# Wide products with a weight's high part, and down blocks placed among the next chunk's pairs, in a one-core decoder layer

## The chip, the cores and the metric

The kernel runs on one core of a Trainium2 chip. The metric is device time in microseconds (us). TensorE (PE in the profile; its weight loads are PEld) multiplies, VectorE (DVE) and ScalarE (ACT) do the elementwise work, GpSimd (POOL) a little of it, and SyncE's queue (SP) issues the DMAs.

## What is computed

A decoder layer in float32, with 512 tokens and 1024 channels: a half-step SwiGLU feed-forward layer (FFN), a token mixer (RG-LRU channels and stick-breaking attention), and a second FFN. Each FFN has 2816 hidden channels:

```python
def _swiglu(x, w_gate, w_up, w_down):
    return (jax.nn.silu(x @ w_gate) * (x @ w_up)) @ w_down

x = x + 0.5 * _swiglu(_rms_norm(x, ffn1_norm[l]), ffn1_w_gate[l], ffn1_w_up[l], ffn1_w_down[l])
... # mixer: proj = h @ w_in; RG-LRU group; attention heads; x = x + y @ w_out
x = x + 0.5 * _swiglu(_rms_norm(x, ffn2_norm[l]), ffn2_w_gate[l], ffn2_w_up[l], ffn2_w_down[l])
```

## The kernel before

**Number format.** Every operand is held as a high part in the rounded format fp32r and a low part (value minus high part). A product is three matmuls: high x high, high x low, low x high (`mm3`, L136 to L138).

**FFN.** The 2816 hidden channels are 22 blocks `f` of 128, taken as 11 pairs `p`, in `CHUNKS` of 6, 6, 6 and 4 blocks. The first three pairs (chunk 0) are plain: 8 k-tiles x 3 matmuls of 512 columns for gate and for up. The pairs 3 to 10 use Strassen's scheme in Winograd's form (`fast`, `matrix`): for a pair's gate matrix and its up matrix, 7 products each of 4 k-tiles x 3 matmuls of 256 columns (L371). Each matrix keeps two PSUM banks, `px` and `py`; a product accumulates on one of them, and behind each product either ScalarE copies the bank to SBUF (`keep`, L389) or VectorE adds it to what was kept (`add`, L394). The 14 products of a pair run in the order "g0 g1 u0 u1 g2 g3 u2 u3 g4 g5 u4 g6 u5 u6".

**Weights of a fast pair.** 1 MB each for gate and up comes in a `raw` buffer (3 buffers, L331). VectorE makes four sums (L334 to L338), ScalarE casts each of four groups to a high part (L357), VectorE subtracts for the low part (L358); high and low parts have 4 buffers each (`wh`, `wl`), which the down weights share.

**Operands of the fast pairs.** `operands()` builds them once for each FFN from the normed input, in four blocks `b` of 8 x 256 columns (L298 to L321), one buffer, high and low parts in separate tiles.

**Down.** At the end of a chunk come 8 down blocks, one for each 128 output channels (L427 to L447): up to 6 x 3 matmuls of 512 columns, then VectorE adds half of the result to `x` (L441).

**Mixer.** Of it the change touches the first projection's bank, and the stretch of the `v` projection: `norm_heads` (head norms of k; `r8k` on POOL, `natk` on VectorE), `yn.rsqrt` (`pst_r` on TensorE, `m_r` on VectorE, `r_r` on POOL), `turn` (transposes `ptk`), and `rnn_out`, which begins with `yn.spread` (four transposes of `r_r` into `pst_r`, L193) and makes `yrh` and `yrl` for the output projection `po`.

**Order.** Tiles and waits come from a scheduler that works at build time: the order on each engine follows the program order, moved by its own model, and then stands. `tc.issue_after(i)` puts the instructions traced in it behind `i` on their engine.

Of the kernel before, what the change touches and what calls it, by code (L numbers as in the profile page):

```python
# [15 lines left out]
P = 128  # L16
T = 512
# [13 lines left out]
TH = T // 2  # L31
WARM = 9
# [14 lines left out]
def hybrid_layer_kernel(  # L47
# [93 lines left out]
    class Normed:  # L141
# [5 lines left out]
        def add(self, xk, gain, j):  # L147
            n = self.name
            h = xpool.tile([P, T], F32R, tag="xh", name=f"xh_{n}{j}", bufs=8)
            high = nc.scalar.activation(h, xk, AF.Copy, scale=gain)  # L150
            l = xpool.tile([P, T], F32R, tag="xl", name=f"xl_{n}{j}", bufs=8)
            nc.vector.scalar_tensor_tensor(
                l, xk, gain, f32(h), op0=ALU.mult, op1=ALU.subtract
            )
            self.h[j], self.l[j] = h, l
            return high
# [11 lines left out]
        def rsqrt(self, dim, tag="y"):  # L168

            n = self.name  # L170
            pt = self.pt = bank(f"pst_{n}", tag)
            for b in range(NB):
                self.summed = nc.tensor.matmul(
                    pt[:, b : b + 1],
                    self.acc[:, b * P : (b + 1) * P],
                    ones[:, 0:1],
                    start=True,
                    stop=True,
                )
            m = stat.tile([P, NB], F32, tag="m", name=f"m_{n}")  # L180
            nc.vector.tensor_scalar(
                m, pt[:, 0:NB], 1.0 / dim, EPS, op0=ALU.mult, op1=ALU.add
            )
# [30 lines left out]
    def ffn(name, xn, wg, wu, wd, first, done):  # L214
        def products(f, between=None, tag="b"):
# [4 lines left out]
            pg, pu = (bank(f"{p}{n}", tag) for p in ("pg", "pu"))  # L220
            each = ((pg, gh, gl), (pu, uh, ul))
            order = [(e, k) for e in each for k in range(KD)]
            if f == 0:
                order = [(e, k) for k in range(KD) for e in each]
            for i, ((pt, wh, wl), k) in enumerate(order):
                s = slice(k * P, (k + 1) * P)
                mm3(pt, wh[:, s], wl[:, s], xn.h[k], xn.l[k], k == 0, k == KD - 1)
                if between and i == KD - 1:
                    between()
            return pg, pu  # L230

        if first:
            ahead = first()
            ahead.append(products(len(ahead), tag="y"))
        else:
            ahead = [products(0), products(1)]
            xn.rsqrt(D)
            ahead.append(products(len(ahead), xn.spread, "y"))
        rb = xn.rb
        with tc.tile_pool(name=f"ffn_{name}", bufs=1, reuse_waits="tile") as fp:  # L240
# [4 lines left out]
            def pair_tiles(p):  # L245
                n = f"{name}{p}"
                g = fp.tile([P, 4, TH], F32, tag="g", name=f"gg{n}", bufs=2)
                u = fp.tile([P, 4, TH], F32, tag="u", name=f"uu{n}")
                return g, u

            def split(u, p, i):

                n = f"{name}{p}"
                h = fp.tile([P, 2, T], F32R, tag=f"hh{i}", name=f"hh{n}")
                l = fp.tile([P, 2, T], F32R, tag=f"hl{i}", name=f"hl{n}")
                for t in range(2):
                    src = flat(u[:, 2 * t : 2 * t + 2, :])
                    nc.scalar.copy(h[:, t, :], src)
                    nc.vector.tensor_sub(l[:, t, :], src, f32(h[:, t, :]))
                return [(h[:, t, :], l[:, t, :]) for t in range(2)]  # L260
# [21 lines left out]
            def operands():  # L282
# [3 lines left out]
                def tiles(n):  # L286
                    if extra[0]:
                        extra[0] -= 1
                        i = extra[0]
                        return [fp.tile([P, 2, TH], F32R, tag=f"x{c}{i}", name=f"x{c}_{n}") for c in "hl"]  # L290
                    return [
                        xpool.tile([P, 2, TH], F32R, tag=f"x{c}", name=f"x{c}_{n}", bufs=8) for c in "hl"
                    ]

                for k in range(KD // 2):
                    n = f"s{name}{k}"

                    b = fp.tile([P, 8, TH], F32, tag="b", name=f"b{n}")  # L298
                    for kk, o in ((2 * k, b[:, 0:2, :][:, ::-1, :]), (2 * k + 1, b[:, 2:4, :])):
                        h, l = (f32(p[kk]).rearrange("p (c t) -> p c t", c=2) for p in (xn.h, xn.l))  # L300
                        nc.vector.tensor_add(o, h, l)
# [8 lines left out]
                    for s in (B11, B22, T2, T4):  # L310
                        if s == T4 and k % 2:
                            h, l, o = *operands.last, 1
                        else:
                            h, l = tiles(f"{n}_{s}")
                            o = 0
                        w = 1 if s == T4 else 2
                        if w == 1:
                            operands.last = h, l
                        src = b[:, s + 1 : s + 1 + w, :]
                        nc.scalar.copy(h[:, o : o + w, :], src)  # L320
                        nc.vector.tensor_sub(l[:, o : o + w, :], src, f32(h[:, o : o + w, :]))  # L321
                        for i in range(w):
                            held[k, s + i] = h[:, o + i, :], l[:, o + i, :]

            def matrix(w, c, p):
# [37 lines left out]
                px, py = (bank(f"p{i}{n}", "b")[:, :TH] for i in "xy")  # L363

                def product(pt, group, half, b, start):
                    wh, wl = get(group)
                    for k in range(KD // 2):
                        s = slice((half * 4 + k) * P, (half * 4 + k + 1) * P)
                        bh, bl = held[k, b]
                        for i, (l, r) in enumerate(((wh, bh), (wh, bl), (wl, bh))):  # L370
                            nc.tensor.matmul(  # L371
                                pt, l[:, s], r, start=start and k == 0 and i == 0,
                                stop=k == KD // 2 - 1 and i == 2, skip_group_check=True,
# [9 lines left out]
            def fast(p, i):  # L383

                g, u = pair_tiles(p)

                def keep(o, c):
                    def after(pt):
                        nc.scalar.copy(o[:, c, :], pt)  # L389
                    return after  # L390

                def add(o, c):
                    def after(pt):
                        nc.vector.tensor_add(o[:, c, :], pt, o[:, c, :])  # L394
                    return after

                def last_gate(pt):
                    nc.scalar.activation(g[:, 2, :], pt, AF.Silu, scale=-1.0)

                both = {}  # L400
                for c, w, o, end in (("g", wg, g, last_gate), ("u", wu, u, keep(u, 2))):

                    after = [keep(o, 0), add(o, 0), keep(o, 1), keep(o, 3), add(o, 3), add(o, 1), end]
                    steps, product = matrix(w, c, p)
                    both[c] = [(product, *z) for z in zip(steps, after)]

                for c in "g0 g1 u0 u1 g2 g3 u2 u3 g4 g5 u4 g6 u5 u6".split():
                    product, step, after = both[c[0]][int(c[1])]
                    product(*step)
                    after(step[0])  # L410
                    if c == "g5":
                        nc.scalar.activation(flat(g[:, 0:2, :]), flat(g[:, 0:2, :]), AF.Silu)
                        nc.scalar.activation(g[:, 3, :], g[:, 3, :], AF.Silu, scale=-1.0)
                nc.vector.tensor_mul(u[:, 0:2, :], u[:, 0:2, :], g[:, 0:2, :])
                nc.vector.scalar_tensor_tensor(
                    u[:, 2:4, :], u[:, 2:4, :], -1.0, g[:, 2:4, :], op0=ALU.mult, op1=ALU.mult
                )
                return split(u, p, i)

            f0 = 0  # L420
            for nf in CHUNKS:
                hs = []
                for i in range(nf // 2):
                    p = f0 // 2 + i
                    hs += (plain if 2 * p < PLAIN else fast)(p, i)
                last = f0 + nf == NF
                for k in range(KD):  # L427
# [20 lines left out]
                if f0 == 0:  # L448
                    operands()
                f0 += nf  # L450
# [216 lines left out]
    def rnn_out():  # L667
        yn.spread(same=True)
# [47 lines left out]
    def norm_heads(n, pts):  # L716
        nats = []
        for b in range(NB):
# [10 lines left out]
            nc.vector.scalar_tensor_tensor(  # L729
                heads(nat),  # L730
                heads(pts[b]),
                rb,
                r.unsqueeze(2).to_broadcast([P, NH, HD]),
                op0=ALU.mult,
                op1=ALU.mult,
            )
# [35 lines left out]
    def gate_and_recur(last):  # L772
# [7 lines left out]
    nk = norm_heads("k", pk)  # L780
# [322 lines left out]
```

## Time and profile before

| | us |
|---|---|
| median of 3 runs (907.25 to 907.58) | 907.39 |
| profiled execution | 907.71 |
| its span | 905.9 |
| TensorE busy | 899.7 |
| VectorE busy | 667.3 |
| ScalarE busy | 450.2 |

The span is that of the instructions; 1.8 us of the profiled execution lie around it. A busy TensorE here is a union of modelled matmul intervals, so its work is better read from the spacing of matmul starts.

### The profile page before, as it was taken

The numbers are of one execution on the slowest core, as the hardware profiler recorded it, in microseconds if no ns is written. First come the engines' busy times: TensorE is split into PE (matmuls) and PEld (weight loads), VectorE is DVE, ScalarE is ACT, GpSimd is POOL, SyncE is SP. The second block draws the span as 40 slices with busy tenths as digits, with TensorE's granted clock in tenths as the row PEclk, the third lists the DMA queues.
The fourth block names the chain that finished last, engine by engine and source line by source line (L and its number), as shares of the span: only waits on it lengthen the run. The fifth ranks groups of instructions, "written<-read, shape, count | busy, mean of one in ns | idle before, by whom it ended". The sixth has DMA issues, their size and how long they took to land.

```text
span 905.9 us, 13634 instructions
## 1 busy us (share of the span) xinstructions
PE 899.7 (99%) x5442; PEld 793.0 (88%) x5442; DVE 667.3 (74%) x998; ACT 450.2 (50%) x757; POOL 70.6 (8%) x60
## 2 busy tenths in 40 slices
PE   9999999999999999999999999999999999999998
PEld 8888899889998998877877677888899989998997
DVE  8699788648865859757698948499688657875663
ACT  6443455335542546365768834443356335642450
POOL 0000000000000005553140002200000000000000
PEclk9999999999999999999999999999999999999999
DMA  8531123512242122322131015322222422242102
GB/s 267 197 136 53 53 94 98 180 49 93 94 163 88 47 94 72 127 93 75 66 115 49 24 47 211 139 61 61 70 94 93 163 70 95 93 163 88 48 24 93
DMA packets 27600, 89.26 MB, mean 99 GB/s; under 512 B 2960, under 2 KB 6288, under 8 KB 23440
## 3 DMA queue, kind: packets, MB, share of 16 engines
q1 hardware_dynamic: 27392, 88.35, 28.8%
q8 instruction: 43, 0.70, 0.3%
q14 instruction: 21, 0.17, 0.1%
q10 hardware_dynamic: 144, 0.03, 0.0%
HBM read 86.28 MB, written 2.10 MB: 98 GB/s over the span
## 4 chain that ended last, share of the span: by engine, by line
PE 93%; DVE 3%; ACT 2%; issue 1%; POOL 1%; DVEq 0%; POOLq 0%; ACTq 0%
PE pxga L371 5%; PE pxgb L371 5%; PE pxub L371 5%; PE pxua L371 5%; PE pdb L138 4%; PE pdb L137 4%; PE pdb L136 4%; PE pda L138 4%; PE pda L137 4%; PE pda L136 4%; PE pygb L371 4%; PE pyga L371 4%; PE pyua L371 4%; PE pyub L371 4%; PE first_p L503 4%; PE po L136 2%
## 5 line engine op out<-in xcount | busy, mean ns | idle before, releaser
L137 PE MATMUL pdb<-hlb,h_db 128*128 128x512 f32 (+2 forms) x180 | 68.9, 386 | 0.0
L138 PE MATMUL pdb<-hhb,l_db 128*128 128x512 f32 (+2 forms) x180 | 68.9, 386 | 0.0
L137 PE MATMUL pda<-hla,h_da 128*128 128x512 f32 x176 | 68.0, 389 | 0.0
L138 PE MATMUL pda<-hha,l_da 128*128 128x512 f32 x176 | 67.9, 389 | 0.0
L136 PE MATMUL pdb<-hhb,h_db 128*128 128x512 f32 (+2 forms) x180 | 67.4, 385 | 0.0
L136 PE MATMUL pda<-hha,h_da 128*128 128x512 f32 x176 | 66.2, 389 | 0.0
L441 DVE SCALAR_TENSOR_TENSOR x<-pdb,x 128x512 f32<-128x512 f32 (+2 forms) x33 | 21.9, 672 | 49.8 <-PE pdb L138 49.8
L441 DVE SCALAR_TENSOR_TENSOR x<-pda,x 128x512 f32<-128x512 f32 x32 | 21.7, 686 | 39.8 <-PE pda L138 39.8
L126 ACT CAST h_da<-r_da 128x768 fp32r<-128x768 f32 (+1 forms) x28 | 24.1, 868 | 48.6 <-PE pda L137 20.8
L126 ACT CAST h_db<-r_db 128x768 fp32r<-128x768 f32 (+1 forms) x28 | 24.3, 868 | 45.2 <-PE pdb L137 23.3
L137 PEld LDWEIGHTS pdb<-hlb,h_db 128*128 128x128 f32 x180 | 33.8, 188 | 6.6
L136 PEld LDWEIGHTS pdb<-hhb,h_db 128*128 128x128 f32 x180 | 33.8, 188 | 6.5
L138 PEld LDWEIGHTS pdb<-hhb,l_db 128*128 128x128 f32 x180 | 33.8, 188 | 6.5
L137 PEld LDWEIGHTS pda<-hla,h_da 128*128 128x128 f32 x176 | 33.0, 188 | 6.7
L138 PEld LDWEIGHTS pda<-hha,l_da 128*128 128x128 f32 x176 | 33.1, 188 | 6.7
L136 PEld LDWEIGHTS pda<-hha,h_da 128*128 128x128 f32 x176 | 33.1, 188 | 6.6
L371 PE MATMUL pxgb<-xh_sb,l_gb 128*128 128x256 f32 x128 | 36.2, 283 | 0.0
L371 PE MATMUL pxga<-xh_sa,l_ga 128*128 128x256 f32 x128 | 36.2, 283 | 0.0
L371 PE MATMUL pxga<-xl_sa,h_ga 128*128 128x256 f32 x128 | 36.2, 283 | 0.0
L371 PE MATMUL pxgb<-xl_sb,h_gb 128*128 128x256 f32 x128 | 36.2, 283 | 0.0
L371 PE MATMUL pxua<-xh_sa,l_ua 128*128 128x256 f32 x128 | 36.2, 283 | 0.0
L371 PE MATMUL pxub<-xh_sb,l_ub 128*128 128x256 f32 x128 | 36.2, 283 | 0.0
(393 smaller groups left out, 3050.5 us busy)
## 6 DMA issues: line engine op xcount, KB each, us to landing
r_da<-in_wd SPq DMA_DIRECT2D x24, 384.0 KB, 3.4
r_db<-in_wd SPq DMA_DIRECT2D x24, 384.0 KB, 3.1
rga<-in_wg SPq DMA_DIRECT2D x8, 1024.0 KB, 5.0
rua<-in_wu SPq DMA_DIRECT2D x8, 1024.0 KB, 4.8
rgb<-in_wg SPq DMA_DIRECT2D x8, 1024.0 KB, 4.9
rub<-in_wu SPq DMA_DIRECT2D x8, 1024.0 KB, 4.8
r_o<-in_w_out SPq DMA_DIRECT2D x8, 512.0 KB, 3.5
r_gb<-in_wg SPq DMA_DIRECT2D x6, 512.0 KB, 3.3
```

The costliest lines, as they stand in the source:

```text
L126: nc.scalar.copy(hi, raw)
L136: nc.tensor.matmul(out_, wh, ah, start=start, stop=False)
L137: nc.tensor.matmul(out_, wh, al, start=False, stop=False)
L138: return nc.tensor.matmul(out_, wl, ah, start=False, stop=stop)
L371: nc.tensor.matmul(pt, l[:, s], r, start=start and k == 0 and i == 0, stop=k == KD // 2 - 1 and i == 2, skip_group_check=True,)
L441: nc.vector.scalar_tensor_tensor(x[k][:, t], pt[:, t], 0.5, x[k][:, t], op0=ALU.mult, op1=ALU.add)
L503: nc.tensor.matmul(pts[i], wp[i][:, s], xp[k], start=k == 0 and wp is hi and xp is n1.h, stop=k == KD - 1 and wp is lo,)
```

## The change

In each FFN, 10 of the 16 fast matrices become wide (`WIDE`: gate of the pairs 3 to 10, up of the pairs 6 and 9). An operand's high and low part now lie side by side, and a wide product is, for each k-tile, one matmul of 512 columns (the weight's high part with both parts) and one of 256 (the weight's low part with the high part) into half of the bank. The two halves are evicted as 512 columns and added once for each matrix by VectorE (1024 columns). SiLU is applied after g6 to all four quarters. The down blocks of the chunks 1 and 2 are issued among the products of the next chunk's first two pairs (`BETWEEN`: before the z-th product of pair i); the first pair of that chunk is split later (`SPLIT`). The blocks `b` move to the `raw` buffers; gate tiles have one buffer, and kept products two shared ones of double size. The second FFN takes the banks of its third block first; the mixer's first projection takes a bank of another group; `norm_heads` of k's last block and `rnn_out` are issued later.

```diff
+BETWEEN = [(0, 2), (0, 5), (0, 8), (0, 11), (1, 0), (1, 2), (1, 4), (1, 6)]
+SPLIT = (1, 8)
+LATE = 3
+WIDE = {p: "gu" if p in (6, 9) else "g" for p in range(PLAIN // 2, NF // 2)}
...
+            third = room(2, "y")
             ahead = [products(0), products(1)]
             xn.rsqrt(D)
-            ahead.append(products(len(ahead), xn.spread, "y"))
+            ahead.append(products(2, xn.spread, third))
...
-                g = fp.tile([P, 4, TH], F32, tag="g", name=f"gg{n}", bufs=2)
-                u = fp.tile([P, 4, TH], F32, tag="u", name=f"uu{n}")
-                return g, u
+                g = fp.tile([P, 4, TH], F32, tag="g", name=f"gg{n}")
+                u = fp.tile([P, 4, 2, TH], F32, tag="o", name=f"uu{n}", bufs=2)
+                return g, u.rearrange("p a b t -> p (a b) t")[:, :4, :]
...
-                    b = fp.tile([P, 8, TH], F32, tag="b", name=f"b{n}")
+                    b = fp.tile([P, 8, TH], F32, tag="raw", name=f"b{n}", bufs=3)
...
+                        with tc.issue_after((split.last if k >= LATE else xn.low).ins):
+                            nc.vector.tensor_add(o, h, l)
...
-                        bh, bl = held[k, b]
-                        for i, (l, r) in enumerate(((wh, bh), (wh, bl), (wl, bh))):
+                        bh, bl = held[k, b][:, 0, :], held[k, b][:, 1, :]
+                        runs = [(wh, flat(held[k, b])), (wl, bh)] if wide else [(wh, bh), (wh, bl), (wl, bh)]
+                        for i, (l, r) in enumerate(runs):
...
+                    o = fp.tile([P, 4, 2, TH], F32, tag="o", name=f"o{c}{n}", bufs=2)
...
+                    after = [keep(0), add(0), keep(1), keep(3), add(3), add(1), keep(2)]
...
+                for z, c in enumerate("g0 g1 u0 u1 g2 g3 u2 u3 g4 g5 u4 g6 u5 u6".split()):
+                    for step in begun.pop((i, z), ()):
+                        step()
...
+                    if c == "g6":
+                        h = src = fp.tile([P, 4, TH], F32, tag="g", name=f"gg{n}")
+                        if both["g"][1]:
+                            nc.vector.tensor_add(h, compact["g"], both["g"][2][:, :, 1, :])
+                        else:
+                            src = compact["g"]
+                        for z0, sign in ((0, 1.0), (2, -1.0)):
+                            nc.scalar.activation(
+                                flat(h[:, z0 : z0 + 2, :]), flat(src[:, z0 : z0 + 2, :]), AF.Silu, scale=sign
+                            )
+                if both["u"][1]:
+                    nc.vector.tensor_add(u, u, both["u"][2][:, :, 1, :])
...
+                for step, at in zip(rest, BETWEEN):
+                    begun.setdefault(at, []).append(step)
...
-        pts = [bank(f"p{n}{j}", "y" if (j, n) == (0, "ga") else "b") for n in ("xr", "ga")]
+        pts = [bank(f"p{n}{j}", "b") for n in ("xr", "ga")]
...
-    nk = norm_heads("k", pk)
+    nk = norm_heads("k", pk, range(3))
+
+    def sums_r(last):
+        yn.rsqrt(DR, "b")
+        nk.extend(norm_heads("k", pk, (3,), yn.mean))
...
-            10: lambda last: yn.rsqrt(DR, "b"),
-            14: lambda last: rnn_out(),
+            10: sums_r,
             19: lambda last: turn("k", nk, (0, 1), last),
             21: lambda last: turn("k", nk, (2,), last),
+            23: rnn_out,
             24: lambda last: turn("k", nk, (3,), last),
```

## Rows read from the trace of the kernel before

**Rows 1.** The page, parts 1 and 2: engines' busy time, and the clock by slices.
```profile
PE 899.7 (99%) x5442; PEld 793.0 (88%) x5442; DVE 667.3 (74%) x998; ACT 450.2 (50%) x757; POOL 70.6 (8%) x60
...
PEclk9999999999999999999999999999999999999999
```

**Rows 2.** The waits of TensorE: who waited, for whom, us, times, longest.
```profile
PE pst_r L193 <- POOL r_r L185: 1.3, 1, 1.3
...
PE pub L136 <- DVE yo L998: 0.5, 1, 0.5
PE ptk L747 <- DVE m_r L181: 0.2, 1, 0.2
```

**Rows 3.** Windows (pairs 3-5, downs, pairs 9-10): us; busy of PE, PEld, DVE, ACT, POOL.
```profile
106.99:167.47 60.48, 60.48 (x501) 60.17 (x500) 50.03 (x79) 33.41 (x61) 0.00 (x0) 1.00 0.33 118
167.47:200.12 32.65, 32.65 (x152) 27.30 (x151) 16.59 (x23) 9.68 (x14) 0.00 (x0) 1.00 0.26 74
...
293.25:333.60 40.35, 40.35 (x331) 40.02 (x331) 28.80 (x43) 21.70 (x38) 0.00 (x0) 1.00 0.14 48
```

**Rows 4.** The chain that ended last: two products of 256 columns.
```profile
106.99 1.44 PE pyga L371 x12
108.43 1.44 PE pxua L371 x12
```

**Rows 5.** Timeline of TensorE: every third start, at 512 and at 128 columns.
```profile
72.76 0.39 PE L136 MATMUL pda<-hha,h_da 128*128 128x512 f32 x1
...
73.44 0.39 PE L136 MATMUL pda<-hha,h_da 128*128 128x512 f32 x1
...
901.92 0.28 PE L136 MATMUL pdb<-hhb,h_db 128*128 128x128 f32 x1
...
902.25 0.28 PE L136 MATMUL pdb<-hhb,h_db 128*128 128x128 f32 x1
```

**Rows 6.** Timeline of VectorE in pair 4: 512, 256 and 1024 columns back to back.
```profile
128.97 0.68 DVE L415 SCALAR_TENSOR_TENSOR uua<-uua,gga 128x512 f32<-128x512 f32 x1
129.57 0.41 DVE L394 TENSOR_TENSOR gga<-pyga,gga 128x256 f32<-128x256 f32 x1
129.91 1.21 DVE L358 TENSOR_TENSOR l_ga<-sga,h_ga 128x1024 fp32r<-128x1024 f32 x1
131.04 1.28 DVE L259 TENSOR_TENSOR hla<-uua,hha 128x512 fp32r<-128x512 f32 x2
```

**Rows 7.** Timeline at the v projection: POOL, VectorE and TensorE.
```profile
462.73 1.64 POOL L726 TENSOR_TENSOR r8k<-m8k,mhalf 128x8 f32<-128x8 f32 x1 [1.48 <-DVE m8k L724]
465.29 1.92 POOL L185 TENSOR_TENSOR r_r<-m_r,mhalf 128x4 f32<-128x4 f32 x1 [0.93 <-DVE m_r L181]
...
464.39 0.75 DVE L729 SCALAR_TENSOR_TENSOR natk<-pk,r_m,r8k 128x512 f32<-128x512 f32 x1 [1.81 <-POOL r8k L726]
...
474.11 1.40 DVE L674 SCALAR_TENSOR_TENSOR yrl<-gel,vec,yrh 128x512 fp32r<-128x512 f32 x2
...
464.64 0.40 PE L138 MATMUL pv<-h_v,xl_m 128*128 128x512 f32 x1
465.29 0.63 PE L747 MATMUL ptk<-ident,natk 128*128 128x128 f32 x4 [0.25 <-DVE m_r L181]
467.26 0.65 PE L193 MATMUL pst_r<-ident,r_r 128*128 128x128 f32 x4 [1.34 <-POOL r_r L185]
...
476.85 0.50 PE L136 MATMUL po<-yrh,h_o 128*128 128x512 f32 x1
```

**Rows 8.** Timeline of VectorE: the last two reads of po before the second FFN.
```profile
554.35 0.68 DVE L998 TENSOR_TENSOR yo<-po,rb_t 128x512 f32<-128x512 f32 x1
...
556.08 0.68 DVE L998 TENSOR_TENSOR yo<-po,rb_t 128x512 f32<-128x512 f32 x1
```

**Rows 9.** Operands: the third block's last instructions; landing time of a pair's weights.
```profile
82.09 1.02 DVE L321 TENSOR_TENSOR xl_sa<-bsa,xh_sa 128x512 fp32r<-128x512 f32 x2
...
rga<-in_wg SPq DMA_DIRECT2D x8, 1024.0 KB, 5.0
```

More of the change, by code (lines that the diff above doesn't have):

```diff
@@ L151, in add @@
             l = xpool.tile([P, T], F32R, tag="xl", name=f"xl_{n}{j}", bufs=8)
-            nc.vector.scalar_tensor_tensor(
+            self.low = nc.vector.scalar_tensor_tensor(
                 l, xk, gain, f32(h), op0=ALU.mult, op1=ALU.subtract
@@ L214, in ffn, with room, products @@
     def ffn(name, xn, wg, wu, wd, first, done):
-        def products(f, between=None, tag="b"):
+        def room(f, tag="b"):
+            return [bank(f"{p}{name}{f}", tag) for p in ("pg", "pu")]
+        def products(f, between=None, pts=None):
             n = f"{name}{f}"
@@ L219, in products @@
             uh, ul = weights(wu[f // 2][:, c : c + KD * P], f"u{n}")
-            pg, pu = (bank(f"{p}{n}", tag) for p in ("pg", "pu"))
+            pg, pu = pts or room(f)
             each = ((pg, gh, gl), (pu, uh, ul))
@@ L233, in ffn @@
             ahead = first()
-            ahead.append(products(len(ahead), tag="y"))
+            ahead.append(products(len(ahead), pts=room(len(ahead), "y")))
         else:
+            third = room(2, "y")
             ahead = [products(0), products(1)]
             xn.rsqrt(D)
-            ahead.append(products(len(ahead), xn.spread, "y"))
+            ahead.append(products(2, xn.spread, third))
         rb = xn.rb
@@ L256, in split @@
                 for t in range(2):
-                    src = flat(u[:, 2 * t : 2 * t + 2, :])
-                    nc.scalar.copy(h[:, t, :], src)
-                    nc.vector.tensor_sub(l[:, t, :], src, f32(h[:, t, :]))
+                    src = u[:, 2 * t : 2 * t + 2, :]
+                    ht, lt = (o[:, t, :].rearrange("p (c t) -> p c t", c=2) for o in (h, l))
+                    nc.scalar.copy(ht, src)
+                    split.last = nc.vector.tensor_sub(lt, src, f32(ht))
                 return [(h[:, t, :], l[:, t, :]) for t in range(2)]
@@ L310, in operands, with matrix @@
                     for s in (B11, B22, T2, T4):
+                        w = 1 if s == T4 else 2
                         if s == T4 and k % 2:
-                            h, l, o = *operands.last, 1
+                            to, both = operands.last, None
                         else:
[L314 to L318, printed above, removed]
-                        src = b[:, s + 1 : s + 1 + w, :]
-                        nc.scalar.copy(h[:, o : o + w, :], src)
-                        nc.vector.tensor_sub(l[:, o : o + w, :], src, f32(h[:, o : o + w, :]))
+                            to, both = tiles(f"{n}_{s}")
+                        src = b[:, s + 1 : s + 1 + w, :]
+                        if both is None or w == 1:
+                            moves = [(to[i], src[:, i, :]) for i in range(w)]
+                            moves = [(o[:, 0, :], o[:, 1, :], z) for o, z in moves]
+                        else:
+                            moves = [(both[:, :, 0, :], both[:, :, 1, :], src)]
+                        for h, l, z in moves:
+                            nc.scalar.copy(h, z)
+                            nc.vector.tensor_sub(l, z, f32(h))
                         for i in range(w):
-                            held[k, s + i] = h[:, o + i, :], l[:, o + i, :]
-            def matrix(w, c, p):
+                            held[k, s + i] = to[i]
+                        if s == T4:
+                            operands.last = to[1:]
+            def matrix(w, c, p, wide):
                 n = f"{c}{name}{p}"
@@ L361, in get @@
                     return hi, lo
-                px, py = (bank(f"p{i}{n}", "b")[:, :TH] for i in "xy")
+                px, py = (bank(f"p{i}{n}", "b")[:, : T if wide else TH] for i in "xy")
                 def product(pt, group, half, b, start):
@@ L368, in product @@
                         s = slice((half * 4 + k) * P, (half * 4 + k + 1) * P)
[L369 to L370 removed]
+                        bh, bl = held[k, b][:, 0, :], held[k, b][:, 1, :]
+                        runs = [(wh, flat(held[k, b])), (wl, bh)] if wide else [(wh, bh), (wh, bl), (wl, bh)]
+                        for i, (l, r) in enumerate(runs):
                             nc.tensor.matmul(
[L372 to L373 removed]
+                                pt[:, : r.shape[1]], l[:, s], r, start=start and k == 0 and i == 0,
+                                stop=k == KD // 2 - 1 and i == len(runs) - 1, skip_group_check=True,
                             )
@@ L381, in matrix, with fast, keep, add @@
                 ], product
[L383 to L408, printed above, removed]
+            def fast(p, i, begun):
+                n = f"{name}{p}"
+                both, compact = {}, {}
+                for c, w in (("g", wg), ("u", wu)):
+                    wide = c in WIDE.get(p, "")
+                    o = fp.tile([P, 4, 2, TH], F32, tag="o", name=f"o{c}{n}", bufs=2)
+                    if wide:
+                        os = [flat(o[:, z]) for z in range(4)]
+                    else:
+                        o = o.rearrange("p a b t -> p (a b) t")
+                        os = [o[:, z, :] for z in range(4)]
+                    compact[c] = o[:, :, 0, :] if wide else o[:, 0:4, :]
+                    def keep(z, os=os):
+                        return lambda pt: nc.scalar.copy(os[z], pt)
+                    def add(z, os=os):
+                        return lambda pt: nc.vector.tensor_add(os[z], pt, os[z])
+                    after = [keep(0), add(0), keep(1), keep(3), add(3), add(1), keep(2)]
+                    steps, product = matrix(w, c, p, wide)
+                    both[c] = [(product, *z) for z in zip(steps, after)], wide, o
+                for z, c in enumerate("g0 g1 u0 u1 g2 g3 u2 u3 g4 g5 u4 g6 u5 u6".split()):
+                    for step in begun.pop((i, z), ()):
+                        step()
+                    product, step, after = both[c[0]][0][int(c[1])]
@@ L420, in ffn, with down, block @@
[L420 to L425, printed above, removed]
+                return lambda: split(h, p, i)
+            def down(f0, nf, hs):
                 last = f0 + nf == NF
-                for k in range(KD):
+                two = None
+                def block(k):
+                    nonlocal two
                     n = f"{name}{f0}_{k}"
@@ L447, in ffn, with put @@
                         done(k)
-                if f0 == 0:
+                return [lambda k=k: block(k) for k in range(KD)]
+            f0, rest = 0, []
+            for nf in CHUNKS:
+                hs = [None] * (nf // 2)
+                begun = {}
+                for step, at in zip(rest, BETWEEN):
+                    begun.setdefault(at, []).append(step)
+                late = bool(rest)
+                for i in range(nf // 2):
+                    p = f0 // 2 + i
+                    if 2 * p < PLAIN:
+                        hs[i] = plain(p, i)
+                        continue
+                    finish = fast(p, i, begun)
+                    def put(i=i, finish=finish):
+                        hs[i] = finish()
+                    if late and i == 0:
+                        begun.setdefault(SPLIT, []).append(put)
+                    else:
+                        put()
+                f0 += nf
+                rest = down(f0 - nf, nf, [part for pair in hs for part in pair])
+                if f0 <= PLAIN or f0 == NF:
+                    for step in rest:
+                        step()
+                    rest = []
+                if f0 == PLAIN:
                     operands()
-                f0 += nf
     psum("ffn_a", b=4, y=4)
@@ L665, in recur, with rnn_out @@
             yn.square(gel[j], j, nc.vector)
-    def rnn_out():
-        yn.spread(same=True)
+    def rnn_out(last):
+        with tc.issue_after(last.ins):
+            yn.spread(same=True)
         for j in range(NJ):
@@ L714, in heads, with norm_heads @@
         return ap.rearrange("p (h d) -> p h d", h=NH)
-    def norm_heads(n, pts):
+    def norm_heads(n, pts, blocks=range(NB), behind=None):
         nats = []
-        for b in range(NB):
+        for b in blocks:
             rb = nm.r[:, b : b + 1]
@@ L728, in norm_heads @@
             nat = rp.tile([P, DR], F32, tag=tag, name=f"nat{n}{b}", bufs=bufs)
[L729 to L736, printed above, removed]
+            with tc.issue_after(behind.ins) if behind else nullcontext():
+                nc.vector.scalar_tensor_tensor(
+                    heads(nat),
+                    heads(pts[b]),
+                    rb,
+                    r.unsqueeze(2).to_broadcast([P, NH, HD]),
+                    op0=ALU.mult,
+                    op1=ALU.mult,
+                )
             nats.append(nat)
```

19 lines of the change are left out of this document (8 added, 11 removed).

## Prediction

> **What bounds the kernel now.** I read the page first. TensorE is busy 99% of the span and its granted clock is full in all 40 slices; VectorE is at 74% [rows 1]. Since matmul ends are modelled, I then asked what TensorE waited for. The reader is to see how little there is: beside the start, three waits of consequence, at the transposes of k, at the spread of `r_r`, and at the first bank of the second FFN [rows 2]. Next come the windows. A chunk's three fast pairs take 60.48 us, which is 504 matmuls at 0.12 us with nothing over, and the downs behind them take 32.65 us, which is 144 at 0.2267 [rows 3]. So between those stretches TensorE has no hole to fill: time there falls only with the number or the columns of matmuls. VectorE is the engine to watch: 50.03 of 60.48 us in the pairs, but only 16.59 of 32.65 in the downs; ScalarE has 33.41 of 60.48 [rows 3].
>
> **The price of a matmul.** Twelve matmuls of 256 columns start 1.44 us apart, so 120.0 ns each [rows 4]. Three of 512 columns take 73.44 - 72.76 = 0.68 us, so 226.7 ns each [rows 5]. At 2.4 GHz 256 columns are 106.7 ns and 512 are 213.3; both leave 13.3 ns, a fixed cost of each instruction. Could 120 ns be the weight load instead? Three matmuls of 128 columns need 0.33 us, 110 ns each [rows 5], where their columns would need 53: that is the load showing, and it lies just below 120. In a wide product a load has a 512-column matmul to hide under every second time, so it binds no sooner than now.
>
> The Trainium skill, page "TensorE: Matmul & The Clock Gate", section "Wait — 56ns, not 53.3ns?", puts the fixed cost of a back-to-back matmul at about 2.5 ns. The 13.3 ns of the rows disagree, and I go by the rows; by the Trainium skill the first term below would be 1.4 us (an estimate: 560 x 2.5 ns).
>
> **Term 1, fewer matmuls.** A wide product replaces 12 x 120.0 = 1440 ns by 4 x 226.7 + 4 x 120.0 = 1387 ns: the same columns, four instructions fewer, 53.3 ns. Wide matrices: 8 gates and 2 ups, 10 in each FFN, 7 products each: 70 x 53.3 ns = 3.73 us, and **7.5 us** in two FFNs. Bounds: nothing, if the fixed cost doesn't fall away when widths alternate; and a second 7.5 us, if the 256-column matmul behind a 512-column one lost its 13.3 ns as well. The 512-column rows, whose loads are covered and which still pay 13.3, speak against that end. I take 7.5.
>
> **Term 2, the transposes of k and the spread.** The last `v` matmul starts at 464.64; without waits the next would start 0.23 later, at 464.87. The transposes start at 465.29 (0.42 late), because a bank comes free only behind `natk`, which ran from 464.39 to 465.14 on VectorE after `r8k` on POOL. The spread starts at 467.26; four transposes take some 0.36 after 465.29, so it is 1.6 late, behind `r_r`, which POOL began only at 465.29 [rows 7]. Together 2.0 us. The change issues the spread after two more steps of 3 x 0.2267 us and puts `r_r` ahead of the last `natk`: the 1.6 us should go. But now the last `natk` queues behind `m_r`, and its `r8k` may queue on POOL behind `r_r` (1.92 us); then the transposes of block 2 wait longer, by up to about 1 us. I take **1.3 us** gained, bounds 0 and 2.0. What is late next is `yrl` for `po`: before, 8.25 us passed from the spread to the last `yrl` (475.51), and `po` started 9.6 after the spread [rows 7]. With the spread after step 23, 9 steps of 0.68 plus a transpose and one score group are about 7.5 us to `po`, and the fourth `yrl` is wanted 2.0 later; 9.5 against 8.25 holds.
>
> **Term 3, banks at the second FFN.** `pub` was held 0.5 us [rows 2] by a read of `po` that ended at 555.03 [rows 8]. With the third block's banks taken first, the first products move to other banks of the mixer. If one of these is the bank read last, the read ends at 556.76 [rows 8], 1.7 us later still, unless gate matmuls fill in. Gain 0.5, loss 1.7: I take **0**. The projection's other bank shows no wait before; nothing.
>
> **Term 4, what VectorE gets.** Back to back, 256 columns occupy VectorE 0.34 us, 512 0.60, 1024 1.13 [rows 6]; the add of 256 columns there reads PSUM, and costs what half of 512 costs in SBUF. A wide matrix turns three adds of 256 into 512 (3 x 0.26 = 0.8) and adds one of 1024 (1.13): 1.93 us, 19.3 in each FFN. ScalarE's four copies double in width; at 33.41 of 60.48 [rows 3] it has room.
>
> For the stretches of one FFN: the pairs 3 to 5 have three wide matrices, so 50.0 + 5.8 = 55.8 us of VectorE in 60.48 - 1.12 = 59.4 of TensorE. The pairs 6 to 8 have four, but the downs now run among them: 50.0 + 16.6 + 7.7 = 74.3 in 60.5 + 32.6 - 1.5 = 91.6. Pairs 9 and 10: 28.8 + 16.6 + 5.8 = 51.2 in 40.4 + 32.6 - 1.1 = 71.9 [rows 3]. Only the first is close. Before, VectorE was idle there for 10.45 us, largely because it had run ahead and the four weight buffers were full; what it falls behind at the end of pair 5 is made up while a down block of 18 x 0.2267 = 4.1 us stands two products into pair 6. A kept bank is needed again two products later (2.8 us), and an add of 0.69 fits. I take **0.5 us** of new waits, bounds 0 and the price of rival 1.
>
> **Parts at nothing.** The moved downs keep their matmuls, their 8 loads each and their adds; on SP they now stand between loads of pair weights, which land in 5.0 us [rows 9] and have a pair's 19.8 us. The late split of a chunk's first pair is not read until the next downs. The operand blocks in `raw` buffers hold back the weights of pair 3: even at the old pace, with one buffer, the third block was done at 83.1 [rows 9]; 5.0 us of landing, a cast (taken as long as the subtraction) and a subtraction of 1.13 end near 90.4, and pair 3 runs from about 106.99 [rows 4]. If that cover were gone each microsecond late would show. One gate buffer instead of two: VectorE works through plain pairs in order anyway.
>
> **Sum.** 907.71 - 7.5 - 1.3 + 0 + 0.5 = 899.4 for the profiled execution; the median lies 0.3 below it, so **899.1 us**.
>
> **Rivals.**
> 1. VectorE becomes the bound in the pairs 3 to 5 (the other side). If the 10.45 us of idle are waits for casts and banks that stay, the stretch takes 55.8 + 10.45 = 66.3 us against 59.4: 6.9 us in each FFN, 13.8 in all, and 912.9. Its room is 59.4 - 55.8 = 3.6 us; it decides when it eats the gain of 8.3, that is 4.2 in each FFN, so from about 7.8 us of idle kept. For it: VectorE's share rises from 83% to 94%. Against: TensorE shows no wait there, so that idle time was slack.
> 2. Small waits at bank turns, operands or the end of the last chunk, some 0.15 us for each wide matrix or a few places of 1 us: 3 us, 902.
> 3. The wide form saves nothing on TensorE, since the fixed cost stays with the load: terms 2 and 4 alone, 906.6, no change to be told. For it: 110 ns at 128 columns. Against: the same 13.3 ns at 512, where the load is covered. By the Trainium skill's 2.5 ns (page "TensorE: Matmul & The Clock Gate") 905.2 would come out.
>
> **How the numbers follow.** Forecast (897 to 901) 0.69, rival 2 (901 to 905) 0.15, rival 3 0.07, rival 1 0.09. A change of 0.2% (1.8 us) is about what can be told from none. Rival 2 is faster throughout and rival 3 mostly the same: faster 0.84, same 0.07, slower 0.09. The range leaves out the rivals 1 and 3. Its low end takes the bounds of the terms 2 and 3 (899.1 - 0.7 - 0.5), no new waits (0.5 less), and a little of term 1's far end: 896.5. Its high end is that of rival 2: 904.5.
>
> **What would show it.** A wide product of 8 matmuls lasting 1.387 us; 560 fewer matmuls; the chunk of pairs 3 to 5 at 59.4 us and pairs 6 to 8 with downs at 91.6; no wait of TensorE at the spread; VectorE near 94% in pairs 3 to 5 without TensorE waiting for `l_g` or `l_u`. I am wrong if wide products keep 1.44 us, or if waits of TensorE on VectorE appear in the pairs or at `pub`.

## The result and the profile after

The changed kernel takes 902.33 us (median of 4 runs, 902.0 to 902.42) against 907.44 for the kernel before (907.25 to 907.58): 5.1 us less, ratio 0.9943 with a 95% interval of 0.9926 to 0.996. Predicted were 899.1 us and a range of 896.5 to 904.5: the direction and the range held, the point lay 3.2 us too low. The profiled execution has a span of 900.6 us and took 902.4.

The page after, part 1 and the clock line of part 2, which answer to [rows 1]:

```profile
PE 895.9 (99%) x4882; PEld 763.0 (85%) x4882; DVE 712.3 (79%) x1032; ACT 469.0 (52%) x771; POOL 71.9 (8%) x60
...
PEclk9999999999999999999999999999999999999999
```

560 matmuls are gone, as the prediction counted. TensorE is still the engine that is hardly ever idle, at a full granted clock in all 40 slices. VectorE has gained 45 us of work (it was to gain 38.6; 9.8 of the 45 stand in experiment 3 too (677.1 us), which has no wide product, so the wide form itself brings 35.2) and TensorE has lost less than 4 us of busy time. So first the question whether TensorE now waits for anything. Its waits after (engine, line, tile, whom for, us in total, times, longest) answer to [rows 2]:

```profile
PE ptk L817 <- DVE natk L799: 0.6, 1, 0.6
PE ptq L817 <- DVE natq L799: 0.2, 1, 0.2
```

Beside the start that is all. The waits for `r_r` and for `yo` at `pub` are gone, and no tile of the FFN pairs is in the list. So what the prediction missed is not a wait of TensorE. The windows, which answer to [rows 3] (pairs 3 to 5; pairs 6 to 8 with the downs of the pairs 3 to 5 among them; pairs 9 and 10 with the downs of 6 to 8):

```profile
105.18:164.60 59.42, 59.42 (x415) 55.40 (x414) 52.55 (x77) 35.85 (x60) 0.00 (x0) 1.00 0.30 107
164.60:255.60 91.00, 91.00 (x527) 80.00 (x526) 73.50 (x104) 45.53 (x74) 0.00 (x0) 1.00 0.31 103
255.60:327.00 71.40, 71.40 (x391) 61.76 (x391) 52.18 (x72) 33.13 (x52) 0.00 (x0) 1.00 0.22 67
```

The marks were set by hand near the forecast lengths (59.4, 91.6, 71.9), and products of neighbouring pairs mix at them, so their widths are no measurement; to be read is that PE is busy for the whole of each window and VectorE is not: 52.55 of 59.42 us, 73.50 of 91.00, 52.18 of 71.40 (predicted 55.8, 74.3, 51.2). What can be measured is the whole stretch of an FFN from the first matmul of pair 3 to the end of its last downs: by the starts of matmuls, 248.4 and 248.9 us before, 246.8 and 247.4 after. So both FFNs together gave 3.1 us, where terms 1 and 4 had 7.0.

What is left is the price of the matmuls themselves. The timeline of TensorE after, one narrow product's first and one wide product's eight matmuls, with the first of the next (start, length, engine, line, tile, form, count):

```profile
107.99 0.40 PE L393 MATMUL pxua<-xb_sa,h_ua 128*128 128x256 f32 x2
...
109.43 0.40 PE L393 MATMUL pyua<-xb_sa,h_ua 128*128 128x256 f32 x2
...
110.88 0.40 PE L393 MATMUL pxga<-xb_sa,h_ga 128*128 128x512 f32 x1
111.11 0.28 PE L393 MATMUL pxga<-xb_sa,l_ga 128*128 128x256 f32 x1
111.23 0.39 PE L393 MATMUL pxga<-xh_sa,h_ga 128*128 128x512 f32 x1
111.45 0.28 PE L393 MATMUL pxga<-xh_sa,l_ga 128*128 128x256 f32 x1
111.57 0.40 PE L393 MATMUL pxga<-xh_sa,h_ga 128*128 128x512 f32 x1
111.80 0.28 PE L393 MATMUL pxga<-xh_sa,l_ga 128*128 128x256 f32 x1
111.92 0.40 PE L393 MATMUL pxga<-xh_sa,h_ga 128*128 128x512 f32 x1
112.16 0.28 PE L393 MATMUL pxga<-xh_sa,l_ga 128*128 128x256 f32 x1
112.28 0.40 PE L393 MATMUL pyga<-xb_sa,h_ga 128*128 128x512 f32 x1
...
113.69 0.40 PE L393 MATMUL pxua<-xb_sa,h_ua 128*128 128x256 f32 x2
```

The narrow product lasts 109.43 - 107.99 = 1.44 us as before; the two wide ones 112.28 - 110.88 = 1.40 and 113.69 - 112.28 = 1.41, not 1.387. Over the 118 wide products whose records are complete the mean from start to start is 1408.8 ns, over 70 narrow ones 1436.7: a wide product saves 28 ns against the narrow ones beside it, and 30 against those of before (1438.8), where 53.3 were predicted. By place, a 512-column matmul is followed after 233.7 to 236.3 ns (226.7 predicted), a 256-column one after 116.2 to 117.7 (120.0 predicted): a pair takes 352 ns in place of 346.7. The columns of 8 matmuls are 1280 ns, so the fixed cost is (1408.8 - 1280) / 8 = 16.1 ns each instead of 13.3.

The mixer's part. POOL, VectorE and TensorE after, at the place of [rows 7]:

```profile
461.31 1.64 POOL L795 TENSOR_TENSOR r8k<-m8k,mhalf 128x8 f32<-128x8 f32 x1 [1.82 <-DVE m_r L188]
462.91 1.01 POOL L192 TENSOR_TENSOR r_r<-m_r,mhalf 128x4 f32<-128x4 f32 x1
...
462.98 0.75 DVE L799 SCALAR_TENSOR_TENSOR natk<-pk,r_m,r8k 128x512 f32<-128x512 f32 x1 [2.09 <-POOL r8k L795]
...
462.88 0.40 PE L145 MATMUL pv<-h_v,xl_m 128*128 128x512 f32 x1
463.88 0.63 PE L817 MATMUL ptk<-ident,natk 128*128 128x128 f32 x4 [0.60 <-DVE natk L799]
...
465.72 0.60 PE L200 MATMUL pst_r<-ident,r_r 128*128 128x128 f32 x4
...
473.87 0.50 PE L143 MATMUL po<-yrh,h_o 128*128 128x512 f32 x1
```

`r_r` now runs right behind `r8k` and ends 1.8 us ahead of the spread, and the spread at 465.72 has no wait. The transposes start 1.00 us after the last `v` matmul, 0.775 more than a matmul needs, where it was 0.42: they wait for the last `natk`, which waits for `r8k`. `po` starts 8.15 us after the spread and waits for no `yrl`.

### The profile page after: what moved, and what is told of

Its sections match the earlier page's. It is cut to its first block, busy times and chain, and to the rows that moved or that the text cites. A ratio compares the mean times of both kernels' runs of the same rounds, so it can differ in the third digit from the quotient of the medians.

```text
span 900.6 us, 12582 instructions
## 1 busy us (share of the span) xinstructions
PE 895.9 (99%) x4882; PEld 763.0 (85%) x4882; DVE 712.3 (79%) x1032; ACT 469.0 (52%) x771; POOL 71.9 (8%) x60
## 4 chain that ended last, share of the span: by engine, by line
PE 93%; DVE 3%; ACT 2%; issue 1%; POOL 1%; POOLq 0%; ACTq 0%
PE pxua L393 5%; PE pxub L393 5%; PE pxgb L393 5%; PE pxga L393 5%; PE pdb L143 4%; PE pdb L145 4%; PE pdb L144 4%; PE pda L143 4%; PE pda L145 4%; PE pda L144 4%; PE pyua L393 4%; PE pyub L393 4%; PE pygb L393 4%; PE pyga L393 4%; PE first_p L571 4%; PE po L143 2%
## 5 line engine op out<-in xcount | busy, mean ns | idle before, releaser
L173 POOL TENSOR_TENSOR sqa_m<-sqa_m,sq_m 128x512 f32<-128x512 f32 x7 | 11.8, 1679 | 311.3 <-ACT sq_m L172 311.0
L135 DVE TENSOR_TENSOR l_da<-r_da,h_da 128x768 fp32r<-128x768 f32 (+1 forms) x28 | 27.8, 991 | 5.0 <-ACT h_da L133 5.0
L135 DVE TENSOR_TENSOR l_db<-r_db,h_db 128x768 fp32r<-128x768 f32 (+1 forms) x28 | 27.7, 992 | 5.0 <-ACT h_db L133 5.0
L377 ACT CAST h_ua<-rua 128x512 fp32r<-128x512 f32 (+1 forms) x24 | 18.3, 764 | 24.1 <-PE pyga L393 11.4
L377 ACT CAST h_ub<-rub 128x512 fp32r<-128x512 f32 (+1 forms) x24 | 18.3, 764 | 23.6 <-PE pygb L393 11.4
L377 ACT CAST h_gb<-rgb 128x512 fp32r<-128x512 f32 (+1 forms) x24 | 18.3, 762 | 22.6 <-PE pdb L144 11.8
```

The lines of the kernel that those rows point to most:

```text
L135: nc.vector.tensor_sub(lo, raw, f32(hi))
L173: (engine or nc.gpsimd).tensor_add(self.acc, self.acc, sq)
L377: nc.scalar.copy(hi[:, to], a)
```

## The experiments

Theory A: the fixed cost of a matmul depends on what stands next to it, and wide products lose part of their gain because 512 and 256 columns alternate. Rivals: B, a 512-column matmul of these products is dearer in any order, for what it reads; P, the 256-column matmul adds into the half of the bank that the 512-column one has just written; and, for the rest of the change, C: the moved downs are what keeps VectorE from holding TensorE up. Experiments 1 to 4 and 5 to 8 each share their runs of the kernel before (907.55 and 907.48), 9 and 10 theirs (907.47).

**1. Grouped.** The four 512-column matmuls of a wide product first, then the four of 256.

```diff
-for k in range(KD // 2):
...
-    runs = [(wh, flat(held[k, b])), (wl, bh)] if wide else [(wh, bh), (wh, bl), (wl, bh)]
...
+if wide:
+    runs = [(wh[:, sl(k)], flat(held[k, b])) for k in ks]
+    runs += [(wl[:, sl(k)], held[k, b][:, 0, :]) for k in ks]
...
```

> In each wide product the four matmuls of 512 columns come first and the four of 256 behind them; the same matmuls, in another order. Theory A (each turn from a 256-column to a 512-column matmul costs about 6 ns net, 9 on the wide one less 3 on the narrow one, and the changed kernel turns at every matmul): a wide product falls from 1.409 to about 1.393 us, and 140 of them give 2.2 us, so 900.1. Theory B (a 512-column matmul on high and low part side by side is itself 9 ns dearer, whatever stands ahead of it): product 1.409 us and 902.3 as it is.

Measured: 900.31 us, ratio 0.9918 (0.9905 to 0.9932), 2.0 us below the change as it stood and near theory A's 900.1. A wide product takes 1397.2 ns (104 of them): the 512-column ones 229.2 to 233.2, those of 256 116.5 to 119.4. The order alone moves the price, so B, which has no place for it, falls.

**2. Twos.** The order 512, 512, 256, 256, twice.

```diff
...
+for k in (0, 2):
+    runs += [(wh[:, sl(q)], flat(held[q, b])) for q in (k, k + 1)]
+    runs += [(wl[:, sl(q)], held[q, b][:, 0, :]) for q in (k, k + 1)]
...
```

> The same in groups of two: 512, 512, 256, 256, so half of the turns go. Theory A: a wide product of about 1.399 us, 1.4 us less in all, 900.9. Theory B: no change, 902.3.

Measured: 899.03 us, ratio 0.9905 (0.9891 to 0.9918). This is the fastest version of the study, 3.3 us below the change and 8.5 below the kernel before. The timeline of TensorE for the same two products as above:

```profile
110.71 0.40 PE L402 MATMUL pxga<-xb_sa,h_ga 128*128 128x512 f32 x1
110.95 0.40 PE L402 MATMUL pxga<-xh_sa,h_ga 128*128 128x512 f32 x1
111.18 0.28 PE L402 MATMUL pxga<-xb_sa,l_ga 128*128 128x256 f32 x1
111.30 0.27 PE L402 MATMUL pxga<-xh_sa,l_ga 128*128 128x256 f32 x1
111.41 0.63 PE L402 MATMUL pxga<-xh_sa,h_ga 128*128 128x512 f32 x2
111.87 0.40 PE L402 MATMUL pxga<-xh_sa,l_ga 128*128 128x256 f32 x2
112.11 0.63 PE L402 MATMUL pyga<-xb_sa,h_ga 128*128 128x512 f32 x2
...
113.50 0.40 PE L402 MATMUL pxua<-xb_sa,h_ua 128*128 128x256 f32 x2
```

112.11 - 110.71 = 1.40 and 113.50 - 112.11 = 1.39 us; the mean over 124 is 1390.7 ns, nearly the 1387 of the prediction. That is 2.5 of the 3.3 us; the rest lies in the moved down blocks, of which one takes 4092.9 ns here and 4119.5 in the changed kernel, with the same 18 matmuls. But theory A expected a price for each turn from 256 to 512, and twos, with two turns, came out cheaper than the grouped order with one. A is right that order sets the price, and wrong in how.

**3. Narrow.** No wide products; all else of the change stays.

```diff
-WIDE = {p: "gu" if p in (6, 9) else "g" for p in range(PLAIN // 2, NF // 2)}
+WIDE = {}
```

> No matrix is wide; all else of the change stays. By the rows of the changed kernel (28 ns saved for each of 140 wide products, some of it lost again at the down blocks that now stand among the products) it should be 3.0 us slower than the changed kernel, 905.3. By the prediction's term 1 (53 ns for each) it would be 7.5 us slower, 909.8.

Measured: 906.07 us, ratio 0.9984 (0.9975 to 0.9993). With 5442 matmuls again the change is worth 1.5 us. So the wide form is worth 906.07 - 902.33 = 3.7 us where 7.5 were predicted: near what the rows of the changed kernel gave (905.3), far from term 1 (909.8).

**4. Downs at the end.** The wide products stay; the down blocks run behind a chunk's pairs, as before the change.

```diff
-if f0 <= PLAIN or f0 == NF:
+if True:
```

> The down blocks stand at the end of their chunk again; the wide products stay. Theory C (VectorE can carry the wide form only because downs among the pairs give it time): in pairs 6 to 8 VectorE has 57.7 us of work in 59 of TensorE without a pause, TensorE waits for low parts 1 to 3 us in each of four chunks, 906 to 914. Rival D (VectorE's idle time in the pairs was slack all along): TensorE waits nowhere, and fewer turns to and from 512 columns give back a few tenths: 901.5 to 902.3.

Measured: 905.49 us, ratio 0.9976 (0.9967 to 0.9986), 3.2 us above the change. TensorE's waits, then its timeline at one of them, then ScalarE's and VectorE's:

```profile
PE pxga L393 <- ACT oga L421: 1.4, 2, 0.7
PE pxgb L393 <- ACT ogb L421: 1.4, 2, 0.7
...
224.80 0.28 PE L393 MATMUL pxga<-xh_sa,l_ga 128*128 128x256 f32 x1
225.75 0.50 PE L393 MATMUL pxga<-xb_sa,h_ga 128*128 128x512 f32 x1 [0.68 <-ACT oga L421]
...
225.12 0.59 ACT L421 COPY oga<-pxga 128x512 f32<-128x512 f32 x1 [0.55 <-PE pxga L393]
...
224.56 0.69 DVE L424 TENSOR_TENSOR oga<-pyga,oga 128x512 f32<-128x512 f32 x1
```

Four waits, at 225.75 and 319.25 us and at the same places of the second FFN, each 0.83 us by starts. Here TensorE runs two products of one bank directly behind each other, and the second waits until ScalarE has copied the bank. The copy itself was not held up: ScalarE had been idle for 0.55 us and began it as the first product ended. What speaks for VectorE stands beside it: it runs back to back from 216 to 228 us, and its add of `pyga` ends at 225.25, 4.7 us after the product in that bank (220.55), so that bank was not free to be taken in between. That this is why the two products stand together is argued, not shown. Rival D (no wait, 901.5 to 902.3) falls. Of C the size holds, the moved downs buy 3.2 us; its own signs, waits for low parts and 906 to 914 us, did not come.

**5. Upper half.** The 256-column matmul of a wide product adds into the half of the bank behind column 256, so that the two halves carry other sums; the sum of the halves is the same.

```diff
+to = pt[:, TH:] if wide and i == 1 else pt[:, : r.shape[1]]
...
-    pt[:, : r.shape[1]], l[:, s], r, start=start and k == 0 and i == 0,
+    to, l[:, s], r, start=start and k == 0 and i == 0,
```

> The order of the changed kernel, 512 and 256 in turn, but the 256-column matmul adds into the upper half of the bank instead of the lower one (the halves are added later, so the sum is the same). Theory P (the dearer matmul comes from writing columns of PSUM that the matmul before has just written): the product falls from 1.409 towards 1.39 us, up to 2.5 us less, 900. Theory A2 (what costs is the change of width from one matmul to the next, wherever it writes): product 1.409 us, 902.3.

Measured: 902.32 us, ratio 0.9945 (0.993 to 0.996); a wide product 1408.7 ns. No change at all: P falls.

**6. Twos, all pairs.** The order of experiment 2, and the up matrices wide in every fast pair.

```diff
+WIDE = {p: "gu" for p in range(PLAIN // 2, NF // 2)}
```

> Order 512, 512, 256, 256, and all 16 fast matrices of each FFN wide: 84 more wide products at 1.391 instead of 1.437 us. Theory T (TensorE stays the bound): 3.9 us less than with that order alone (899.0), 895.1. Rival V (VectorE binds in pairs 3 to 5, where it gets 50.0 + 6 x 1.93 = 61.6 us of work for 58 us of TensorE): TensorE waits there, at least 3 us in each FFN, and the gain is eaten: 899 to 904.

Measured: 911.87 us, ratio 1.005 (1.0035 to 1.0065): slower than the kernel before, with 896 matmuls fewer. TensorE's waits, the clock line, and TensorE behind its last wait:

```profile
PE pda L143 <- ACT hha L271: 2.4, 1, 2.4
...
PE pxga L402 <- ACT oga L430: 1.4, 2, 0.7
...
PE pyga L402 <- ACT oga L430: 1.2, 2, 1.0
...
PEclk9999999999999999999999999999999999999998
...
887.60 2.08 PE L143 MATMUL pdb<-hhb,h_db 128*128 128x512 f32 x4 [2.42 <-ACT hhb L271]
889.47 0.63 PE L144 MATMUL pdb<-hlb,h_db 128*128 128x512 f32 x1
```

The second FFN has the same waits, so they are some 10 us, and behind the last of them matmuls of 512 columns start 0.43 us apart for 3.2 us, that is at 1.2 GHz (granted clock 0.50 from 887.5 to 890.9): 1.6 us more. Neither expectation named this time (895.1; 899 to 904). It is rival 1 of the prediction in kind, waits on work that VectorE's load makes late, met when that load is raised by 12 matrices more; but of 6.2 us by starts in each FFN only 1.7 lie in the pairs 3 to 5, where rival 1 and rival V had put them, and 2.6 stand ahead of the last downs. With 0.1 us more behind each wait, where the first matmul is followed after 0.34 us, and with the clock they make up some 15 us, less 3.9 saved; of the 12.6 by which the profiled execution lies over that of experiment 2, about 1.3 stay open.

**7. The old mixer.** `norm_heads` and `rnn_out` in the order of before; the rest as changed.

```diff
-    with tc.issue_after(last.ins):
+    with tc.issue_after(last.ins) if last else nullcontext():
...
-nk = norm_heads("k", pk, range(3))
+nk = norm_heads("k", pk)
...
-10: sums_r,
+10: lambda last: yn.rsqrt(DR, "b"),
+14: lambda last: rnn_out(None),
...
-23: rnn_out,
```

> Only the order at the v projection goes back to that before (norm_heads of k in one go, rnn_out after step 14). Term 2 as the two traces show it (the waits at the transposes and the spread were 0.42 + 1.55 us, and 0.78 remains): 1.2 us slower than the changed kernel, 903.5. Rival: the 2.0 us come back whole or not at all, 904.3 or 902.3.

Measured: 903.98 us, ratio 0.9962 (0.9947 to 0.9976), 1.65 us above the change, between the 903.5 of the traces and the rival's 904.3. Its waits of TensorE show the two of [rows 2] at `pst_r` and `ptk` again:

```profile
PE pst_r L200 <- POOL r_r L192: 1.4, 1, 1.4
...
PE ptk L817 <- DVE m_r L188: 0.6, 1, 0.6
```

**8. Third block's banks later.** They are taken where the kernel before takes them.

```diff
-third = room(2, "y")
 ahead = [products(0), products(1)]
 xn.rsqrt(D)
-ahead.append(products(2, xn.spread, third))
+ahead.append(products(2, xn.spread, room(2, "y")))
```

> Only the banks of the second FFN's third block are taken where they were before. As the two traces show it (a wait of 0.66 us at pub that is gone): 0.7 us slower than the changed kernel, 903.0. Rival (the wait went because the blocks now come at other times): no change, 902.3.

Measured: 903.54 us, ratio 0.9956 (0.9941 to 0.997), 1.2 above the change by medians, 0.7 by the spans of the profiled executions (901.3 against 900.6). The rival (no change) falls; the wait is back:

```profile
PE pub L143 <- DVE yo L1072: 0.5, 1, 0.5
```

**9. Twos, most pairs.** As 2, with the up matrices wide in the pairs 6, 7, 9 and 10, where downs run among the pairs.

```diff
-WIDE = {p: "gu" if p in (6, 9) else "g" for p in range(PLAIN // 2, NF // 2)}
+WIDE = {p: "gu" if p in (6, 7, 9, 10) else "g" for p in range(PLAIN // 2, NF // 2)}
```

> In e2's order, the up matrices of pairs 7 and 10 become wide too (pairs 6, 7, 9, 10; those of 8 and of 3 to 5 stay narrow): 2 more in each FFN, 28 more products, 112 fewer matmuls. If VectorE keeps up where downs run among the pairs, each saves 1436.7 - 1390.7 = 46 ns, 1.3 us in all: 897.7. If VectorE is already at its bound there, waits of TensorE for its adds appear in these pairs as in e6, and the time rises: 900 or more.

Measured: 909.28 us, ratio 1.0026 (1.0016 to 1.0036): 10 us worse than experiment 2, from two more wide matrices in each FFN. TensorE's waits; then VectorE, ScalarE and TensorE at the end of the first FFN's pairs:

```profile
PE pda L143 <- ACT hha L271: 2.4, 1, 2.4
...
PE pyga L402 <- ACT oga L430: 1.0, 1, 1.0
...
PE pxga L402 <- ACT oga L430: 0.7, 1, 0.7
...
335.25 1.22 DVE L460 TENSOR_TENSOR oua<-oua 128x1024 f32<-128x1024 f32 x1
336.50 0.69 DVE L461 TENSOR_TENSOR gga<-oua,gga 128x512 f32<-128x512 f32 x1
...
337.28 1.22 ACT L271 CAST hha<-gga 128x512 fp32r<-128x512 f32 x2 [2.73 <-DVE gga L461]
...
337.95 1.19 PE L143 MATMUL pda<-hha,h_da 128*128 128x512 f32 x4 [2.42 <-ACT hha L271]
```

The hope fell and the rival's time held, though the releasers named are ScalarE's copies and casts. Where the last pair's up matrix is wide, the add of its halves on VectorE (L460), the products with the gate (L461, L462) and the cast behind them stand between TensorE's last product and the last downs, and nothing is left to fill 2.4 us; some 90 us earlier two bank turns come late (0.7 and 1.0). By starts the three cost 4.5 us in each FFN, and 0.1 more behind each of them, less 1.3 saved in all: 8.4 over experiment 2, and its profiled execution is 8.5 over (907.38 against 898.9). Its nine runs go from 907.38 to 911.05, and the time follows the mean granted clock: 0.999 in the profiled one, 0.998 in three from 908.77 to 909.03, 0.997 at 909.28, 0.996 in four from 910.30 to 911.05. So what the others lose beyond the waits goes with a lower clock, as in experiment 6; where in these runs it fell is not shown.

**10. The turn inside.** The order 512, 256, 256, 512, twice.

```diff
+for k in (0, 2):
+    x, y = [[(wh[:, sl(q)], flat(held[q, b])), (wl[:, sl(q)], held[q, b][:, 0, :])] for q in (k, k + 1)]
+    runs += [x[0], x[1], y[1], y[0]]
```

> A wide product in the order 512, 256, 256, 512, twice: the stream has runs of two equal widths as in e2 (the 512 at a product's end is followed by that at the next one's beginning), but the two matmuls of a run of 256 now follow the widest gap between their weights' use, and the run of 512 goes across the end of a product. If only the length of the runs counts, a product takes 1391 ns and the kernel 899.0 as e2. If what counts is where in a product the first 512 stands, it lies nearer to the alternating order: about 1400 ns and 901.

Measured: 900.1 us, ratio 0.992 (0.9907 to 0.9934); a wide product 1400.2 ns (92 of them). Runs of two as in experiment 2, yet 9.5 ns dearer: the length of a run of equal widths is not what counts, or not alone. Unlike experiment 2, this order has each operand's 512 and 256 columns side by side, as the alternating one does; that this is the cause was not tried, and experiment 1, which has them apart too, takes 1397.2.

## Why the prediction was right, and where it was off

- **What bounds the kernel** held: TensorE has next to no hole, and the time falls with its instructions. (The first window of [rows 3] begins one product late, at 106.99 for 105.40; its sum is not touched by that.)
- **Term 1** was mis-sized, and is most of the miss: 3.7 us by experiment 3 where 7.5 stood. The step that failed is that a matmul's fixed cost is 13.3 ns in any company. It had been read from streams of one width, [rows 4] and [rows 5], and carried over to an alternating one, where it is 16.1. The lower bound, "nothing, if the fixed cost doesn't fall away when widths alternate", had named the place; rival 3, which took that bound whole, did not come.
- **The moved downs**, put at nothing because they keep their matmuls, do cost: a block of 18 matmuls takes 4119.5 ns among the pairs (24 blocks that stand whole) instead of 18 x 226.7 = 4080, some 40 ns in each of 32 blocks, 1.3 us. Most of it is not the wide form's: with no wide product, in experiment 3, a block takes 4108.9 ns.
- **The sum**: (53.3 - 30) x 140 = 3.3 us and 1.3 us were lost, 4.6 in all; the FFN stretches show 7.5 - 3.1 = 4.4. Given back were 0.7 for the banks and 0.5 for waits that did not come, which leaves the 3.2 us by which the point lay too low.
- **Term 2**: 1.3 predicted; 0.775 left of 0.42 + 1.6 is 1.2 gained, and experiment 7 gives 1.65 for the whole old order. Its details held: the spread without a wait, the transposes later behind the last `natk`, `yrl` in time. `r8k` did not queue behind `r_r`; it ran ahead of it.
- **Term 3**: nothing predicted, 0.7 gained by the spans of experiment 8 (1.2 by medians), above the upper bound of 0.5; the feared loss of 1.7 did not come.
- **Term 4**: 0.5 predicted, none seen. VectorE's load came out 45 us instead of 38.6, yet TensorE waits for it nowhere in the FFN pairs. Experiment 4 gives the moved downs a worth of 3.2 us, as the argument about room for VectorE would have it, though how VectorE brings its waits about is not shown; experiments 6 and 9 show how near waits of rival 1's kind were: two matrices more in each FFN are enough.
- **Rival 2** named the time, 902, but for small waits, and there are none. Its time was met by another cause. So there was luck in the range: the time lies outside the band of the forecast itself (897 to 901) and in that of rival 2 (901 to 905), whose end had set the range's 904.5.

## What to carry to other kernels

Where TensorE is full, fewer and wider matmuls do pay, but the price of one must be read from a stream in the same order of widths; when widths are mixed, try orders, for here the same eight matmuls cost 1408.8 ns alternating and 1390.7 in twos. An engine at 80% that feeds a full one has less room than its share says: look at the last tile of each stage, where nothing covers it, before giving it more. Work with little need of that engine, put among the stretches that need it most, can make the room: moving the downs there was worth 3.2 us here.

## What the runs showed of the hardware that was not expected

The fixed cost of a 256- or 512-column fp32r matmul over its columns at 2.4 GHz was 13.2 ns in the narrow products of before, 13.8 in twos, 14.7 in fours, 15.0 with the turn inside, 16.1 alternating. Why is open: neither the bank's half (5) nor the length of runs (1, 2, 10) explains it, and the order also changes which weight load runs beside which matmul, which no run here holds fixed: a rival that stays untested. It is nothing that only wide products have. In experiment 3, which has none, the first matmuls of a down block behind 256-column ones are dear as well, two in 0.47 us where two take 0.453 in [rows 5]:

```profile
185.26 0.40 PE L143 MATMUL pda<-hha,h_da 128*128 128x512 f32 x1
...
185.73 0.39 PE L145 MATMUL pda<-hha,l_da 128*128 128x512 f32 x1
```

Over the 28 blocks of that run that stand whole, the first five are followed after 233.6, 235.6, 228.8, 231.9 and 231.0 ns, those from the sixth on after 226.5 to 227.2: what a 512-column matmul costs more behind 256-column ones wears off within five there. The Trainium skill, page "TensorE: Matmul & The Clock Gate", section "Wait — 56ns, not 53.3ns?", has one fixed cost of about 2.5 ns for a back-to-back matmul at 2.4 GHz; no stream of these products shows one so small, and the wide form gave 3.7 us where that figure would have given 1.4.

After the second wait of 2.42 us in experiment 6 TensorE ran for 3.2 us with 0.43 us for each 512-column matmul, which is 1.2 GHz, before it went back to 0.23; after the first wait of that length in the same run (at 339.09, granted clock 1.00 behind it), and after the one at 337.95 in experiment 9, it did not, four matmuls taking 338.98 - 337.95 = 1.03 us. One wait can thus cost 1.6 us more than it shows, or not.
